# Seven half-size products for eight in the up-projections of a block's two feed-forward layers

## The chip, the cores and the metric

The program runs on one core of a Trainium2 chip. The metric is the device time of one execution in microseconds (us), the median of three runs. The engines of the core work side by side, and each takes its own instructions strictly in the order of its queue: TensorE (PE in the profile, its weight loads PEld) multiplies matrices into PSUM banks; ScalarE (ACT) and VectorE (DVE) work element by element on SBUF and PSUM; GpSimd (POOL) does the same on SBUF here; SyncE (SP) issues the transfers of weights.

## The reference

Two transformer blocks over one sequence of 512 tokens and 1024 features, all in float32. The change concerns the second block, whose two feed-forward layers are

```python
D_FF = 2816
def swiglu(x, w_gu, w_down):
    g, u = jnp.split(x @ w_gu, 2, axis=-1)
    return (jax.nn.silu(g) * u) @ w_down

def second_block(x, ...):
    x = x + FFN_RES_WEIGHT * swiglu(rmsnorm_2(x, norm_ffn1_g[l]), ffn1_w_gu[l], ffn1_w_down[l])
    x = x + hybrid_mixer(rmsnorm_2(x, norm_mix_g[l]), w_in[l], ...)
    x = x + FFN_RES_WEIGHT * swiglu(rmsnorm_2(x, norm_ffn2_g[l]), ffn2_w_gu[l], ffn2_w_down[l])
    return rmsnorm_2(x, final_norm_g)
```

`x @ w_gu` is the up-projection (512 x 1024 by 1024 x 5632), the product with `w_down` the down-projection.

## The kernel before

**Products.** Activations stand as [feature, token], eight tiles of 128 features. A float32 value is held as two float32r parts, `h` and `l`, with h + l the value, and a product is three matmuls per tile of 128 input features: h by h, h by l, l by h (lines 274, 275 and 277 of `fm`). The weights are the stationary operand, the activations the moving one of 512 tokens (256 where a step runs by token halves).

**Weights.** `w_dma` loads blocks of 1024 x 256 (1 MB, tile `raw`, two buffers) on SP's queue. `w_split` cuts each in four chunks of 128 x 512: ACT copies a chunk into `wh` (line 186), DVE subtracts to get `wl` (line 187); there are three buffers of split blocks. A block's split is issued when `w_done` has freed a buffer.

**Feed-forward layer** (`ffn`). The 22 tiles of hidden features go in three rounds of 6, 8 and 8 (`ROUNDS`). In a round, each pair of tiles takes two blocks of weights, one of the g columns (called a here) and one of the u columns (v): 2 x 2 x 8 x 3 = 96 matmuls of 512 tokens. When a's bank is full ACT takes silu of it (line 946), when v's is full DVE multiplies with it (line 968), and `split` puts the result into the two parts `mh`, `ml` (ACT line 315, DVE line 318). Four down blocks then follow and add to x (DVE line 632), the last two of the last round by token halves with the next norm's squares: ACT squares, POOL adds them up (line 337). The first pair of a layer runs by token halves while the norm is still being finished; the other ten pairs of each layer run as written here.

**Order.** Instructions are issued in program order, and an engine runs them in that order. Side work (splits of weights, norms) is written as generators; `Weave` mixes their steps into the main stream by a clock `t` that counts the TensorE time that has been emitted. A generator says after each step how much of that clock is to pass until its next (1.6 for a chunk of a split, `MISC_D[0]`). Where the main stream needs a block whose split is not yet all issued, `wait` issues what is left of it there and then.

## Time and profile before

| | us |
|---|---|
| Runs | 2775.51, 2780.48, 2782.68; median 2780.48 |
| Span of the profiled execution, first to last instruction | 2771.8 |
| Median less that span | 8.7 |
| Busy: PE, PEld, DVE, ACT, POOL | 2725.3, 2309.7, 1466.6, 1052.3, 280.1 |
| Six stretches with the pairs in question (20 pairs) | 446.1 |

The profiled execution is one execution on the chip; its own time is its span and what lies around it, which is taken as the 8.7 us by which the median of the runs is above the span. The page gives busy times of whole engines. What an edit costs is read from a stretch (a table of busy times by engine) and from the timeline, which shows single instructions with start and duration. The start of one matmul after another is the rate of TensorE; its listed duration overlaps with the next.

### The profile page before, as it was taken

To read this page: it belongs to the slowest core of one execution; us is meant where nothing else is said; L and a number is where in the kernel's file an instruction comes from. 1 tells how busy PE (TensorE), PEld (TensorE's weight loads), DVE (VectorE), ACT (ScalarE), POOL (GpSimd) and SP (SyncE) were. 2 spreads that over 40 slices of the span, in tenths; PEclk is the share of its full clock that TensorE was granted. 3 is DMA by queue.
4 is the path that set the end of the run, shared out by engine and by line. 5 is a ranking of instruction groups with operands and counts; after the bars stand their busy time and mean duration, and the time that the engine had idled before them with its cause. 6 is when DMAs were issued, how large, how long until landed. Compare 5 with 4: busy or idle time off the path is not lost.

```text
span 2771.8 us, 36529 instructions
## 1 busy us (share of the span) xinstructions
PE 2725.3 (98%) x14561; PEld 2309.7 (83%) x14561; DVE 1466.6 (53%) x2791; ACT 1052.3 (38%) x2044; POOL 280.1 (10%) x404
## 2 busy tenths in 40 slices
PE   6999999999999999999999999999999999999999
PEld 5988898888978888888889888897878987988888
DVE  7866567767544896544446333353455235533333
ACT  3323343323323895433334232343256333422222
POOL 3111110000101792000011000010000000100001
PEclk9999999999999999999999999999999999999999
DMA  7542126555231001233222322323433233232221
GB/s 251 185 152 71 59 92 198 175 175 182 79 107 61 1 2 64 97 100 106 91 92 84 99 91 97 102 63 108 105 78 88 54 89 105 77 101 96 92 92 60
DMA packets 254183, 278.69 MB, mean 101 GB/s; under 512 B 12952, under 2 KB 228397, under 8 KB 254013
## 3 DMA queue, kind: packets, MB, share of 16 engines
q1 hardware_dynamic: 226283, 233.21, 27.0%
q10 hardware_dynamic: 27730, 43.14, 4.8%
q8 instruction: 115, 1.88, 0.3%
q14 instruction: 55, 0.45, 0.1%
HBM read 274.23 MB, written 2.10 MB: 100 GB/s over the span
## 4 chain that ended last, share of the span: by engine, by line
PE 92%; DVE 4%; ACT 1%; POOL 1%; issue 1%; ACTq 0%; DMA 0%; DVEq 0%; POOLq 0%
PE pg L274 26%; PE pg L275 26%; PE pg L277 26%; PE pa L733 2%; PE pg L306 1%; PE pg L304 1%; PE pg L305 1%; PE pa L1279 1%; DVE w L546 1%; PE pa L1322 1%; PE pa L360 1%; PE pg L1238 1%; PE pg L1237 1%; PE pa L1048 1%; PE pa L344 1%
## 5 line engine op out<-in xcount | busy, mean ns | idle before, releaser
L187 DVE TENSOR_TENSOR wl<-raw,wh 128x512 fp32r<-128x512 f32 x842 | 571.1, 711 | 426.6 <-ACT wh L186 425.0
L274 PE MATMUL pg<-b,wh 128*128 128x512 f32 (+1 forms) x1856 | 672.6, 363 | 1.0 <-DVE w L968 1.0
L275 PE MATMUL pg<-b,wl 128*128 128x512 f32 (+1 forms) x1856 | 667.2, 360 | 0.0
L274 PE MATMUL pg<-hTh,wh 128*128 128x512 f32 (+3 forms) x1672 | 638.4, 383 | 1.8 <-ACT hTh L315 1.2
L275 PE MATMUL pg<-hTh,wl 128*128 128x512 f32 (+3 forms) x1672 | 633.1, 380 | 0.7 <-DVE wl L187 0.7
L277 PE MATMUL pg<-hTl,wh 128*128 128x512 f32 (+3 forms) x1672 | 621.5, 376 | 0.0
L186 ACT ACTIVATE wh<-raw 128x512 fp32r<-128x512 f32 x842 | 477.6, 619 | 279.8 <-PE pg L277 173.4
L277 PE MATMUL pg<-b,wh 128*128 128x512 f32 (+1 forms) x1472 | 523.9, 358 | 0.0
L275 PEld LDWEIGHTS pg<-b,wl 128*128 128x128 f32 x1856 | 348.8, 188 | 56.4
L274 PEld LDWEIGHTS pg<-b,wh 128*128 128x128 f32 x1856 | 348.6, 188 | 56.5 <-DVE w L968 1.4
L274 PEld LDWEIGHTS pg<-hTh,wh 128*128 128x128 f32 (+2 forms) x1672 | 313.4, 187 | 72.5 <-issue 4.6
L277 PEld LDWEIGHTS pg<-hTl,wh 128*128 128x128 f32 (+2 forms) x1672 | 310.4, 188 | 66.8 <-DVE hTl L318 0.4
L275 PEld LDWEIGHTS pg<-hTh,wl 128*128 128x128 f32 (+2 forms) x1672 | 313.5, 187 | 60.0 <-DVE wl L187 1.1
L277 PEld LDWEIGHTS pg<-b,wh 128*128 128x128 f32 x1472 | 275.2, 188 | 42.9
L337 POOL TENSOR_TENSOR w<-w,w 128x256 f32<-128x256 f32 (+1 forms) x78 | 78.1, 1006 | 1797.6 <-ACT w L336 1797.1
L315 ACT ACTIVATE b<-w 128x512 fp32r<-128x512 f32 (+1 forms) x112 | 67.4, 602 | 380.2 <-DVE w L968 314.8
L277 PE MATMUL pg<-hTh,wh 128*128 128x512 f32 (+1 forms) x384 | 142.9, 378 | 0.0
L968 DVE TENSOR_TENSOR w<-w,pg 128x512 f32<-128x512 f32 (+1 forms) x96 | 61.5, 641 | 146.7 <-PE pg L277 146.2
L318 DVE TENSOR_TENSOR b<-w,b 128x512 fp32r<-128x512 f32 (+1 forms) x112 | 73.3, 654 | 74.8 <-ACT b L315 74.8
L546 DVE SCALAR_TENSOR_TENSOR w<-w,cact,w 128x512 f32<-128x512 f32 x140 | 106.4, 760 | 4.2 <-DMA w<-in_ada_w_dram 3.6
L952 DVE SCALAR_TENSOR_TENSOR w<-pg,PT,w 128x511 f32<-128x511 f32 (+1 forms) x96 | 67.6, 704 | 75.6 <-ACT w L950 73.9
L632 DVE SCALAR_TENSOR_TENSOR x<-pg,mod,x 128x512 f32<-128x512 f32 (+1 forms) x80 | 50.5, 640 | 95.7 <-PE pg L277 90.7
(378 smaller groups left out, 2898.0 us busy)
## 6 DMA issues: line engine op xcount, KB each, us to landing
raw<-in_ffn_w_up_dram SPq DMA_DIRECT2D x44, 1024.0 KB
raw<-in_ffn_w_gu_dram SPq DMA_DIRECT2D x44, 1024.0 KB
w<-in_ada_w_dram ACTq DMA_DIRECT2D x160, 256.0 KB
raw<-in_ffn_w_down_dram SPq DMA_DIRECT2D x32, 1024.0 KB
raw<-in_w_in_dram SPq DMA_DIRECT2D x32, 1024.0 KB
raw<-in_hg_w_in_dram SPq DMA_DIRECT2D x16, 1024.0 KB
raw<-in_ffn_w_down_dram SPq DMA_DIRECT2D x16, 768.0 KB
raw<-in_nsa_w_in_dram SPq DMA_DIRECT2D x10, 1024.0 KB
```

The source lines that it names most:

```text
L186: nc.scalar.activation(h[:, k:e], raw[:, k:e], AF.Copy)
L187: nc.vector.tensor_tensor(l[:, k:e], raw[:, k:e], h[:, k:e].bitcast(F32), op=OP.subtract)
L274: mm(p[:mw, :n], h[:, k, c], xh[:, k, lo:hi], start=k == 0, stop=False)
L275: mm(p[:mw, :n], l[:, k, c], xh[:, k, lo:hi], start=False, stop=False)
L277: mm(p[:mw, :n], h[:, j, c], xl[:, j, lo:hi], start=False, stop=j == nk - 1)
L315: self.nc.scalar.activation(h, src, AF.Copy)
L318: self.nc.vector.tensor_tensor(l, src, h.bitcast(F32), op=OP.subtract)
L337: nc.gpsimd.tensor_tensor(acc[0][:, lo:hi], acc[0][:, lo:hi], sq[:, lo:hi], op=OP.add)
L546: nc.vector.scalar_tensor_tensor(acc, w, self.cact[:, k:k + 1], acc, op0=OP.mult, op1=OP.add)
L733: mm(p[:, c, :n], s["k"][:, cc], q, start=True, stop=True)
L952: nc.vector.scalar_tensor_tensor(c[:, lo + d:hi], p[:, :n - d], w(j), c[:, lo + d:hi], op0=OP.mult, op1=OP.add)
L968: nc.vector.tensor_tensor(s_[:, lo:hi], s_[:, lo:hi], p[:, :hi - lo], op=OP.mult)
```

## The change

In the ten pairs after the first of each of the second block's two feed-forward layers, the two blocks of a pair are no longer multiplied one by one. The matrix of weights is seen as 2 x 2 (a and v columns by the two halves of the 1024 input features), the activations as 2 x 2 (the halves of the input features by the two halves of the tokens), and the product is formed in Winograd's variant of Strassen's way, with seven products of quarter size in place of eight. One step per product, in the order A11, S1, S2, A12, S3, S4, A22 (`FACTORS`, names of the weight factor): 2 x 4 x 3 = 24 matmuls of 256 tokens each (`fm_fast`, lines 475 to 477), 168 for a pair of blocks (called a group below).

What comes with it:

- Sums of weights on POOL: X = a21 + a22 (line 218), a11 - a21 in place (line 219), X - a11 once S1 is split (line 240), a12 - X once S2 is split (line 243). X (`wsum`, 128 x 1024) has one buffer, so the next group's X is formed once S4 is split.
- Splits of weights on ACT and DVE (lines 267 and 268): seven factors of 2 chunks, 14 chunks for a group, where the pair had 8.
- Sums of activations once per layer (`fast_inputs`): POOL lines 425 and 445, DVE lines 444, 446 and 447, then splits, into the tiles b2 and b3.
- Evacuation of a group: three PSUM copies on ACT (lines 1121, 1124, 1127), four adds or products with a PSUM operand on DVE (lines 1129, 1132, 1134, 1139), two silu on ACT (lines 1130, 1135), one product on POOL (line 1136), then two splits (lines 485, 488). PSUM tile A takes four of the products one after the other, E two, F one.
- In the whole kernel: weights are loaded and split by half blocks, with six half buffers of each kind; one more transient tile; a smaller scratch for the issuing of transfers. As many bytes of weights are loaded.

The diff, cut to its core (edits that only pass on half blocks are left out):

```diff
-RAW_BUFS, HL_BUFS, W2_BUFS = 2, 3, 10
+RAW_BUFS, HL_BUFS, W2_BUFS = 6, 6, 11
+SUM_D, CHUNK_D, T_D = 2.6, 1.2, 1.2
...
+    def w_sums(self):
...
+        g = self.groups[self.g_sums]
+        tt = self.nc.gpsimd.tensor_tensor
+        a11, a21, a22 = (self.w_raw[g["load"] + i] for i in range(3))
+        g["X"] = self.t([128, 4, 256], "wsum")
+        tt(g["X"], a21, a22, op=OP.add)
+        tt(a21, a11, a21, op=OP.subtract)
+        g["sums"] = True
...
+    def w_after(self, p):
+        k = p["kind"]
+        if k == "raw":
+            return self.raw_free(p["load"])
+        g = p["g"]
+        tt = self.nc.gpsimd.tensor_tensor
+        raw = lambda i: self.w_raw[g["load"] + i]
+        if k == "S1":
+            tt(g["X"], g["X"], raw(0), op=OP.subtract)
+            self.raw_free(g["load"])
+        elif k == "S2":
+            tt(g["X"], raw(3), g["X"], op=OP.subtract)
+        elif k == "S4":
+            self.g_free += 1
+            self.w_sums()
+        elif k != "A11":
+            self.raw_free(g["load"] + dict(S3=1, A22=2, A12=3)[k])
...
+        p = self.pieces[i]
+        while p["kind"] != "raw" and p["kind"][0] == "S" and not p["g"]["sums"]:
+            yield None
+        if p["kind"] in ("S2", "S4"):
+            yield SUM_D
+        nk, ncol = p["nk"], p["n"]
+        src = self.w_source(p)
+        h = self.t([128, 4, 256], "wh", HL_BUFS, F32R)
+        l = self.t([128, 4, 256], "wl", HL_BUFS, F32R)
         self.w_hl[i] = (h, l)
         step = max(1, 512 // ncol)
         for k in range(0, nk, step):
             e = min(nk, k + step)
-            nc.scalar.activation(h[:, k:e], raw[:, k:e], AF.Copy)
-            nc.vector.tensor_tensor(l[:, k:e], raw[:, k:e], h[:, k:e].bitcast(F32), op=OP.subtract)
+            nc.scalar.activation(h[:, k:e, :ncol], src[:, k:e, :ncol], AF.Copy)
+            nc.vector.tensor_tensor(l[:, k:e, :ncol], src[:, k:e, :ncol], h[:, k:e, :ncol].bitcast(F32),
+                                    op=OP.subtract)
             if slow:
-                yield MISC_D[0]
+                yield MISC_D[0] if p["kind"] == "raw" else CHUNK_D
         self.w_split_i += 1
-        self.w_dma()
+        self.w_after(p)
...
+    def fast_inputs(self, X, tags, first, second):
+        nc = self.nc
+        xh, xl = X
+        th, tl = self.big(tags[0], F32R), self.big(tags[1], F32R)
+        two = lambda t: t.rearrange("p (i t) -> p i t", t=256)
+        def whole(k, lo, f):
+            nc.gpsimd.tensor_tensor(two(f), xh[:, k::4, lo:lo + 256].bitcast(F32), xl[:, k::4, lo:lo + 256].bitcast(F32),
+                                    op=OP.add)
+            return f
+        def run():
+            yield from self.wv.wait_in(first)
+            yield 1.5
+            left = []
+            store = self.t([128, 1024], "hmask")
+            for k in range(4):
+                left.append(whole(k, 0, store[:, k * 512:k * 512 + 512] if k < 2 else self.w2()))
+                yield T_D
+            yield from self.wv.wait_in(second)
+            yield 0.5
+            for k in range(4):
+                r, q = whole(k, 256, self.w2()), left[k]
+                yield T_D
+                a, b = self.w2(), self.w2()
+                tt = nc.vector.tensor_tensor
+                tt(a[:, 0:256], r[:, 0:256], q[:, 0:256], op=OP.subtract)
+                nc.gpsimd.tensor_tensor(a[:, 256:512], r[:, 256:512], r[:, 0:256], op=OP.subtract)
+                tt(b[:, 0:256], r[:, 256:512], a[:, 0:256], op=OP.subtract)
+                tt(b[:, 256:512], q[:, 256:512], b[:, 0:256], op=OP.subtract)
+                for i, f in enumerate((a, b)):
+                    self.split(th[:, i * 4 + k, :], tl[:, i * 4 + k, :], f)
+                    yield T_D
+        return (th, tl), self.wv.spawn(run())
+    def fm_fast(self, X, T, blocks, after):
+        mm = self.nc.tensor.matmul
+        x = lambda k0, lo: tuple((t, k0, lo) for t in X)
+        t = lambda k0, lo: tuple((u, k0, lo) for u in T)
+        steps = (("A11", x(0, 0), "A"), ("S1", t(0, 0), "E"), ("S2", t(4, 0), "A"), ("A12", x(4, 0), "F"),
+                 ("S3", t(0, 256), "A"), ("S4", x(4, 256), "E"), ("A22", t(4, 256), "A"))
+        self.fast_banks = self.fast_banks or [self.pg() for _ in range(4)]
+        self.fast_banks[:2] = self.fast_banks[1::-1]
+        place = dict(zip("AEF", self.fast_banks[1:]))
+        banks = {}
+        for p, (name, (h_, l_), b) in zip(self.w_get(*blocks), steps):
+            assert self.pieces[p]["kind"] == name
+            h, l = self.w_piece(p)
+            first = b not in banks
+            if first:
+                banks[b] = place[b]
+            for m in range(2):
+                o = banks[b][:, m * 256:m * 256 + 256]
+                c = slice(m * 128, m * 128 + 128)
+                for k in range(4):
+                    xh, xl = (u[:, k0 + k, lo:lo + 256] for u, k0, lo in (h_, l_))
+                    mm(o, h[:, k, c], xh, start=first and k == 0 and m == 0, stop=False, skip_group_check=True)
+                    mm(o, h[:, k, c], xl, start=False, stop=False, skip_group_check=True)
+                    mm(o, l[:, k, c], xh, start=False, stop=k == 3 and m == 1, skip_group_check=True)
+                    self.wv.pe(3 * 256 * 0.000424)
+            self.w_done((p,), 0.1)
+            after(name, banks)
...
+                out += [("S", *pair)] if fast and t else pair
...
+        def fast_group(a, t):
+            c = {}
+            f = slice(t - a, t - a + 2)
+            two = lambda w: w.rearrange("p (m t) -> p m t", t=256)
+            def late(lo, src):
+                yield 1.2
+                self.split(mh[:, f, lo:lo + 256], ml[:, f, lo:lo + 256], two(src))
+            def after(step, banks):
+                A, E, F = (banks.get(n) for n in "AEF")
+                if step == "A11":
+                    c["1"] = self.w2()
+                    nc.scalar.activation(c["1"], A, AF.Copy)
+                elif step == "S1":
+                    c["5"] = self.w2()
+                    nc.scalar.activation(c["5"], E, AF.Copy)
+                elif step == "S2":
+                    c["2"] = self.w2()
+                    nc.scalar.activation(c["2"], A, AF.Copy)
+                elif step == "A12":
+                    nc.vector.tensor_tensor(c["1"], c["1"], F, op=OP.add)
+                    nc.scalar.activation(c["1"], c["1"], AF.Silu)
+                elif step == "S3":
+                    nc.vector.tensor_tensor(c["5"], c["5"], A, op=OP.add)
+                elif step == "S4":
+                    nc.vector.tensor_tensor(c["2"], c["2"], E, op=OP.add)
+                    nc.scalar.activation(c["2"], c["2"], AF.Silu)
+                    nc.gpsimd.tensor_tensor(c["2"], c["2"], c["5"], op=OP.mult)
+                    pend.append(self.wv.spawn(late(256, c["2"]), 1.2))
+                else:
+                    nc.vector.tensor_tensor(c["1"], c["1"], A, op=OP.mult)
+                    pend.append(self.wv.spawn(late(0, c["1"])))
+            self.fm_fast(X, T, ((up, 0, 8, t * 128, 256), (up, 0, 8, DFF + t * 128, 256)), after)
...
+                if fast and not first:
+                    self.wv.wait(t_task)
+                    fast_group(a, t)
+                    continue
...
+            for task in pend:
+                self.wv.wait(task)
+            pend.clear()
+            self.fast_banks = None
...
+                 tags=("b2", "b3"))
```

**ACT's queue, second round of the first of the two layers, third pair, before.** Between two evacuations (line 946) ACT splits blocks for later pairs; `wh_13609` and `wh_13675` belong to the next pair.

```order
L186 ACTIVATE wh_13609<-raw_13524 128x512 x2
L946 ACTIVATE w_1604_13635<-pg_13602 128x512 [waits PE_49]
L186 ACTIVATE wh_13609<-raw_13524 128x512
L946 ACTIVATE w_1607_13666<-pg_13637 128x512 [waits PE_49]
L186 ACTIVATE wh_13675<-raw_13591 128x512 [waits DMAHW7_49,Activation_49]
L186 ACTIVATE wh_13675<-raw_13591 128x512 x2
L315 ACTIVATE b_1574_13330<-w_1604_13635 128x512 [waits DVE_49]
L186 ACTIVATE wh_13675<-raw_13591 128x512
L315 ACTIVATE b_1574_13330<-w_1607_13666 128x512 [waits DVE_49]
```

**The same place after, from the end of one group (its splits, line 485) through steps A11, S1 and S2 of the next.** `wsum_14473` is X of that next group; `wh_14549` is the split of S1, `wh_14609` that of S2, `pg` the PSUM tiles.

```order
L485 ACTIVATE b_1949_14071<-w_1983_14406 128x2x256 [waits Pool_49]
L267 ACTIVATE wh_14549<-wsum_14473 128x512 [waits Activation_49]
L485 ACTIVATE b_1949_14071<-w_1976_14338 128x2x256 [waits DVE_49]
L267 ACTIVATE wh_14549<-wsum_14473 128x512
L1121 ACTIVATE w_1998_14578<-pg_14073 128x512 [waits PE_49]
L1124 ACTIVATE w_2000_14607<-pg_14075 128x512 [waits PE_49]
L267 ACTIVATE wh_14609<-wsum_14473 128x512 [waits Pool_49]
L267 ACTIVATE wh_14609<-wsum_14473 128x512
L267 ACTIVATE wh_14619<-raw_14440 128x512 [waits DMAHW4_49,Activation_49]
L267 ACTIVATE wh_14619<-raw_14440 128x512
```

Between the S1 and the S2 step the copy of S1's product (line 1124, waiting for PE) now stands ahead of the split of S2's factor, which the very next step reads; before, the splits that stand here are read by the pair after.

**DVE's queue, before, in the same pair.** `wl_13676` belongs to the next pair's second block.

```order
L187 TENSOR_TENSOR wl_13676<-raw_13591,wh_13675 128x512 [waits DMAHW7_49,PE_49,Activation_49]
L187 TENSOR_TENSOR wl_13676<-raw_13591,wh_13675 128x512 [waits Activation_49] x2
L968 TENSOR_TENSOR w_1604_13635<-w_1604_13635,pg_13668 128x512 [waits PE_49]
L318 TENSOR_TENSOR b_1575_13331<-w_1604_13635,b_1574_13330 128x512 [waits Activation_49]
L187 TENSOR_TENSOR wl_13676<-raw_13591,wh_13675 128x512 [waits Activation_49]
L968 TENSOR_TENSOR w_1607_13666<-w_1607_13666,pg_13704 128x512 [waits PE_49]
L318 TENSOR_TENSOR b_1575_13331<-w_1607_13666,b_1574_13330 128x512 [waits Activation_49]
```

**The same place after, steps S3 to A22 of one group.** `wl_14708` is the lower part of S4's factor, `wl_14720` of A22's, `wl_14757` of the next group's A11.

```order
L268 TENSOR_TENSOR wl_14652<-raw_14271,wh_14651 128x512 [waits Activation_49] x2
L1129 TENSOR_TENSOR w_1998_14578<-w_1998_14578,pg_14076 128x512 [waits PE_49]
L1132 TENSOR_TENSOR w_2000_14607<-w_2000_14607,pg_14073 128x512 [waits PE_49]
L268 TENSOR_TENSOR wl_14708<-wsum_14473,wh_14707 128x512 [waits Activation_49] x2
L268 TENSOR_TENSOR wl_14720<-raw_14341,wh_14719 128x512 [waits DMAHW3_49,Activation_49]
L268 TENSOR_TENSOR wl_14720<-raw_14341,wh_14719 128x512 [waits Activation_49]
L1134 TENSOR_TENSOR w_2005_14646<-w_2005_14646,pg_14075 128x512 [waits PE_49]
L268 TENSOR_TENSOR wl_14757<-raw_14509,wh_14756 128x512 [waits DMAHW5_49,DVE_49,Activation_49]
L268 TENSOR_TENSOR wl_14757<-raw_14509,wh_14756 128x512 [waits Activation_49]
```

The add of S3's product (line 1132, waiting for PE) now stands ahead of the subtraction that makes S4's lower part, and S4 is the next step.

**POOL's queue, before, around the same layer: the last of the additions for the norm ahead of it, and the first for the norm behind it.** Nothing stands between them.

```order
L337 TENSOR_TENSOR w_1445_12072<-w_1445_12072,w_1494_12466 128x256 [waits Activation_49]
L337 TENSOR_TENSOR w_1443_12070<-w_1443_12070,w_1498_12511 128x256 [waits Activation_49]
L337 TENSOR_TENSOR w_1445_12072<-w_1445_12072,w_1499_12514 128x256 [waits Activation_49,Pool_49]
L337 TENSOR_TENSOR w_1695_14664<-w_1695_14664,w_1704_14733 128x512 [waits PE_49,Activation_49,Pool_49]
L337 TENSOR_TENSOR w_1695_14664<-w_1695_14664,w_1708_14770 128x512 [waits Activation_49,Pool_49]
L337 TENSOR_TENSOR w_1695_14664<-w_1695_14664,w_1711_14803 128x512 [waits Activation_49,Pool_49]
```

**After, one group's sums and its product.** `wsum` is X, `raw` the loaded quarter blocks.

```order
L218 TENSOR_TENSOR wsum_14473<-raw_14271,raw_14341 128x1024 [waits DMAHW2_49,DMAHW3_49,DVE_49,Pool_49]
L219 TENSOR_TENSOR raw_14271<-raw_14269,raw_14271 128x1024 [waits DMAHW1_49,Pool_49]
L1136 TENSOR_TENSOR w_1983_14406<-w_1983_14406,w_1978_14367 128x512 [waits Activation_49]
L240 TENSOR_TENSOR wsum_14473<-wsum_14473,raw_14269 128x1024 [waits DVE_49]
L243 TENSOR_TENSOR wsum_14473<-raw_14440,wsum_14473 128x1024 [waits DMAHW4_49,DVE_49,Pool_49]
L218 TENSOR_TENSOR wsum_14713<-raw_14511,raw_14581 128x1024 [waits DMAHW6_49,DMAHW7_49,DVE_49,Pool_49]
L219 TENSOR_TENSOR raw_14511<-raw_14509,raw_14511 128x1024 [waits DMAHW5_49,Pool_49]
```

Five instructions of POOL for each group stand where there was none, and the product of line 1136 stands behind the next group's two sums.

## Rows read from the trace of the kernel before

**Rows 1.** The page: busy by engine; clock; chain; the matmuls by lower parts (last: idle).

```profile
PE 2725.3 (98%) x14561; PEld 2309.7 (83%) x14561; DVE 1466.6 (53%) x2791; ACT 1052.3 (38%) x2044; POOL 280.1 (10%) x404
PEclk9999999999999999999999999999999999999999
PE 92%; DVE 4%; ACT 1%; POOL 1%; issue 1%; ACTq 0%; DMA 0%; DVEq 0%; POOLq 0%
L275 PE MATMUL pg<-hTh,wl 128*128 128x512 f32 (+3 forms) x1672 | 633.1, 380 | 0.7 <-DVE wl L187 0.7
```

**Rows 2.** Busy by stretch; columns PE, PEld, DVE, ACT, POOL, clock, DMA share, GB/s.

```profile
1577.10:1666.20 89.10, 89.10 (x385) 72.01 (x384) 30.39 (x47) 25.97 (x47) 0.00 (x0) 1.00 0.30 98
sum 446.10, PE 446.10 PEld 360.19 DVE 152.24 ACT 130.40 POOL 0.00; mean PE 74.35 PEld 60.03 DVE 25.37 ACT 21.73 POOL 0.00
```

**Rows 3.** Timeline of PE: start, us, what; matmuls of 512 tokens, four pairs.

```profile
1577.08 0.39 PE L274 MATMUL pg<-hTh,wh 128*128 128x512 f32 x1
...
1666.25 0.40 PE L274 MATMUL pg<-b,wh 128*128 128x512 f32 x1
```

**Rows 4.** Timeline of PE: matmuls of 256 tokens, first and last of two runs.

```profile
1448.21 0.28 PE L274 MATMUL pg<-b,wh 128*128 128x256 f32 x1
...
1461.52 0.28 PE L277 MATMUL pg<-b,wh 128*128 128x256 f32 x1
...
1490.07 0.29 PE L275 MATMUL pg<-hTh,wl 128*128 128x256 f32 x1
...
1492.59 0.29 PE L275 MATMUL pg<-hTh,wl 128*128 128x256 f32 x1
```

**Rows 5.** Timeline of ACT in the second round, from a pair's start.

```profile
1582.85 0.60 ACT L946 ACTIVATE w<-pg 128x512 f32<-128x512 f32 x1 [4.42 <-PE pg L277]
1583.35 1.14 ACT L186 ACTIVATE wh<-raw 128x512 fp32r<-128x512 f32 x2
...
1588.92 1.66 ACT L186 ACTIVATE wh<-raw 128x512 fp32r<-128x512 f32 x3
```

**Rows 6.** Timeline of DVE, the same stretch.

```profile
1577.28 0.69 DVE L632 SCALAR_TENSOR_TENSOR x<-pg,x 128x512 f32<-128x512 f32 x1 [2.23 <-PE pg L277]
1577.95 1.30 DVE L187 TENSOR_TENSOR wl<-raw,wh 128x512 fp32r<-128x512 f32 x2
1589.57 1.90 DVE L187 TENSOR_TENSOR wl<-raw,wh 128x512 fp32r<-128x512 f32 x3 [4.28 <-ACT wh L186]
1594.00 0.69 DVE L968 TENSOR_TENSOR w<-w,pg 128x512 f32<-128x512 f32 x1 [2.53 <-PE pg L277]
1595.99 0.68 DVE L187 TENSOR_TENSOR wl<-raw,wh 128x512 fp32r<-128x512 f32 x1
```

**Rows 7.** Timelines of ACT and DVE: from a copy's start to the subtraction behind it.

```profile
1661.60 0.63 ACT L315 ACTIVATE b<-w 128x512 fp32r<-128x512 f32 x1 [4.14 <-DVE w L968]
...
1662.26 0.69 DVE L318 TENSOR_TENSOR b<-w,b 128x512 fp32r<-128x512 f32 x1 [0.70 <-ACT b L315]
```

**Rows 8.** Timeline of POOL, elementwise instructions of two sizes.

```profile
40.69 6.17 POOL L542 TENSOR_TENSOR w<-w,w 128x512 f32<-128x512 f32 x4 [15.74 <-ACT w L540]
722.21 1.30 POOL L337 TENSOR_TENSOR w<-w,w 128x512 f32<-128x512 f32 x1 [4.20 <-ACT w L336]
1068.63 1.30 POOL L337 TENSOR_TENSOR w<-w,w 128x512 f32<-128x512 f32 x1 [16.76 <-ACT w L336]
1454.51 1.45 POOL L337 TENSOR_TENSOR w<-w,w 128x256 f32<-128x256 f32 x2 [1.53 <-ACT w L336]
```

**Rows 9.** Timeline of DVE beside and behind those instructions of POOL.

```profile
42.36 3.37 DVE L546 SCALAR_TENSOR_TENSOR w<-b,cact,w 128x512 f32<-128x512 f32 x2
47.18 5.47 DVE L546 SCALAR_TENSOR_TENSOR w<-b,cact,w 128x512 f32<-128x512 f32 x7
722.62 1.43 DVE L187 TENSOR_TENSOR wl<-raw,wh 128x512 fp32r<-128x512 f32 x1 [1.22 <-ACT wh L186]
1069.10 2.58 DVE L187 TENSOR_TENSOR wl<-raw,wh 128x512 fp32r<-128x512 f32 x3 [1.22 <-ACT wh L186]
```

## What the change is predicted to do

> **What bounds the kernel now.** I read the page first, then the six stretches that hold the pairs to be changed, then single instructions in them, then each pair of engines that would have to share work.
>
> The page says TensorE: busy for 98% of the span, 92% of the chain of waits, the full clock in each of the forty slices [rows 1]. In the six stretches this is complete: 446.10 us long, PE busy for 446.10, DVE for 152.24, ACT for 130.40, POOL not at all [rows 2]. Four pairs take 1666.25 - 1577.08 = 89.17 us [rows 3], so a pair takes 22.3 and a matmul of 512 tokens 0.2322. Here a microsecond of TensorE is one of the kernel, and there is room on the other engines: per pair some 14.7 us of DVE's and 15.8 of ACT's. What the change spends there is free only while it is done before TensorE asks for it. So I ask of each added instruction what it stands behind in its queue, and which step reads it.
>
> **The change part by part** (each term for both layers together; negative is faster).
>
> *Multiplications.* A matmul of 256 tokens starts every (1461.52 - 1448.21) / 113 = 0.1178 us with the operand b, and every (1492.59 - 1490.07) / 21 = 0.1200 with hTh and hTl [rows 4]. Four of the seven steps read the sums in b2 and b3, three read hTh and hTl: a mean of 0.1187, and 168 x 0.1187 = 19.95 us for a group. That is 2.36 under the pair, not the 2.79 of an eighth. Twenty groups: **-47.2**, between -43.0 (all at 0.1200) and -50.4 (all at 0.1178).
>
> A page makes this larger. "TensorE: Matmul & The Clock Gate" of the Trainium skill, section on the back-to-back issue gap, gives 262 cycles for 256 columns, an estimate of 0.109 us and 18.3 for a group; the rows of this kernel show 0.118 to 0.120, and I go by them. By the page the term would be about -80.
>
> *The wait ahead of S2.* A group's splits are paced at 7 x 2 x 1.2 + 2 x 2.6 = 22.0 us of the clock that issues them, while a group's matmuls advance that clock by 168 x 256 x 0.000424 = 18.2. The lead of the splits is lost by 3.8 per group, and the queue after the change shows where it ends: from a round's second or third group on, S2's split is issued at the end of S1, behind the copy of S1's product (line 1124). That copy starts 0.20 us after a step's last matmul (1577.08 to 1577.28 on DVE [rows 3, 6]), holds ACT for 0.50 (1582.85 to the next at 1583.35 [rows 5]), then S2's first chunk takes 0.62 (1.14 for two at a pitch of 0.52 [rows 5]) and 0.04 to cross. TensorE stands for about 1.4 us. The lower part, 0.69 more on DVE after 0.03 [rows 6, 7], is read two matmuls (0.24) later: 1.85. I take 1.7.
>
> *The wait ahead of S4.* Here DVE's add of S3's product (line 1132) is ahead of the subtraction for S4's lower part: 0.20 + 0.67 (1594.00 is 0.69 alone; two in a row take 0.61 to 0.67 each [rows 6]) + 0.69 - 0.24 = 1.3. I take 1.35. These two waits are 3.05 per steady group, more than the 2.36 gained: a steady group is 23.0 before anything is said of POOL.
>
> *POOL's chain to A11 and S1.* X has one buffer, so the next group's two sums begin when S4 is split, about 0.7 after S4 starts. POOL takes 1.30 for 128x512 and 0.72 for 128x256 [rows 8], so 128x1024 is about 2.45 by that slope, and 3.1 by the slowed row (6.17 for four, 1.54 each [rows 8]); the two sums take 4.9 to 6.2, the product of line 1136 behind them 1.3 to 1.54. Behind it ACT has the split of line 485 (0.6) ahead of S1's first chunk (0.6), and DVE has line 488 (0.7) and line 1139 ahead of its lower part (0.7). From S4's start that is 0.7 + 4.9 + 1.3 + 0.6 + 0.6 + 0.7 = 8.8 at the least and 11.5 at the most (DVE at its slowed times as well). S1 starts three steps after S4, at 3 x 2.85 = 8.55. So 0.3 to 3 us are waited; I take 1.9. The sum of line 240 (2.45 from S1's split) ends about when the copy of line 1124 does, and that of line 243 has two steps of room: both at nothing, with line 240 at 0.6 if POOL runs at its slowed rate.
>
> A steady group is then 19.95 + 1.7 + 1.35 + 1.9 = **24.9** against 22.3. Ten groups are steady (in each layer three of round two, two of round three): 10 x 4.95 = **+49.5**, between 10 x 3.05 = 30.5 and 10 x 7 = 70. Six (the second group of the first round and the first ones after it, as the lead runs out) have one of the two fixed waits: 6 x 1.35 = **+8.1**, from 0 to 18. Two have none.
>
> *First group of each layer.* Its S1 reads the sums of activations. Their last two thirds of work stand on POOL behind the sum of line 240: 2.45 + 3 x 0.72 + 2 x 1.30 = 7.2, then a DVE add and a split (0.4 + 0.6 + 0.7), and A11's step covers 2.85: 6.0. Twice: **+12**, from 6 to 16.
>
> *Ends of rounds.* The down blocks read `mh` and `ml`, whose last parts come from the product on POOL and line 1139; before, one split followed the last product. About 1.2 for each of six rounds (a split's two halves, 0.6 and 0.7): **+7**, from 0 to 12.
>
> *Norms.* The sums of the next layer's weights (two of 2.45 to 3.1) stand on POOL ahead of additions that the norm waits for, in two places: **+3**, from 0 to 6.
>
> *Everything else.* Half blocks, six buffers and the input sums' other parts leave the rest of the kernel with the same chunks and the same bytes. All idle time of the matmuls with lower parts that a split ended was 0.7 us [rows 1], so at most about that is to be gained; one wait of the S2 kind in each of three stages would cost 5. I take 0.
>
> Sum: -47.2 + 49.5 + 8.1 + 12 + 7 + 3 = **+32.4**. On the span of 2771.8 this gives 2804.2; the profiled execution's own time is 8.7 more, which is the median of the runs by the way it was taken, so 2804.2 + 8.7 = **2812.9, rounded to 2813 us**.
>
> **The rivals.**
>
> *A. The gain stays.* If ACT and DVE run ahead of TensorE by more than the issuing order says, the waits shrink. For it: DVE and ACT are idle for two thirds of these stretches [rows 2]. Against it: lines 1124 and 1132 wait for TensorE's step to end, and no engine passes an instruction of its own queue. With the fixed waits at a third and the rest at its lower bounds: -47.2 + 10 + 6 = -31, **2749 us**.
>
> *B. The two fixed waits alone.* POOL's chain fits in its three steps, since its lower estimate is only 0.3 over. -47.2 + 30.5 + 8.1 + 12 = +3.4, **2784 us**: the gain and the waits cancel.
>
> *C. POOL and DVE hold each other up.* One mechanism, at one place: an elementwise instruction of DVE with two SBUF operands stands nearly still while POOL runs one. It is in the trace. A subtraction of 0.69 took 1.43 beside a POOL instruction of 1.30, three that take 1.90 took 2.58 with 0.83 of them beside POOL, and two that take 0.78 each took 3.37, while POOL's own went from 1.30 to 1.54 [rows 6, 8, 9]. POOL would be busy for 4 x 2.45 + 1.3 = 11.1 of each group's 22, and DVE has 16 such instructions in a group. It decides where the subtractions for S2, S4 and S1 fall beside a sum: each then takes 0.75 more, and the chain to S1 is at its upper end. A steady group is 24.9 + 2 x 0.75 + 0.6 = 27.0 and the others about 1 more: 2813 + 21 + 10 = **2844 us**. Half of it is in my forecast by the middle values.
>
> "GPSIMD Engine Reference" of the Trainium skill, sections on specifications and engine selection, says the same in general: POOL shares its SBUF interfaces with DVE where DVE has two SBUF inputs, and elementwise work belongs on DVE. The trace agrees (1.43 for 0.69). It speaks against this change, and stands behind rival C.
>
> *D. It isn't seven eighths in time.* If a matmul of 256 tokens were held back by its weight load, 168 of them would save nothing. The rows that run so show 0.118 to 0.120 over 113 and 21 in a row [rows 4], so I give this no more than 0.02; at the 0.133 where nothing is gained the time would be 2813 + 47 = 2860 us.
>
> **How the numbers follow.** Forecast 0.45 (own range 2795 to 2830); A 0.17 (2733 to 2765); B 0.20 (2772 to 2795); C 0.16 (2830 to 2870); D 0.02. About 0.3%, 8.3 us, is what a measurement here can tell from no change: faster means under 2772, slower over 2789. Faster: A, and a seventh of B, 0.20. Same: 0.13, most of B. Slower: 0.67. To leave out no more than 2 in 10 the range reaches into the upper third of A and the lower half of C: 2755 to 2850.
>
> **What would show it.** In the changed kernel's stretches: starts of line 475 to 477 every 0.118 to 0.120 us inside a step; a gap of PE of 1.4 to 1.9 ahead of S2, ended by the split of line 267 or 268, with line 1124 just ahead of that on ACT; 1.3 ahead of S4 ended by line 268 behind line 1132; a gap ahead of S1 ended by the same lines behind POOL's line 1136; 4 to 8 us ahead of the first group's S1, ended by line 485 or 488. DVE's subtractions at 0.69 where POOL is idle and 1.4 beside it. The six stretches together near 446 + 32 = 478 us. I am wrong if the gaps ahead of S2 and S4 are under 0.5 us, if POOL's 128x1024 is far from 2.5 to 3.1, or if time appears in stages without these groups.

## The result: 70 us slower, and what the profile after shows

The changed kernel takes 2851.6 us (median of 4 runs, 2846.7 to 2854.4) against 2781.1 for the kernel before beside it: a ratio of 1.0261, 95% interval 1.0245 to 1.0276. The prediction was slower, 2813 us, with 2755 to 2850 as its range. The direction held; the loss was 70.5 us, not 32.4, and came out just above the range, where rival C (2844) stood. The two profiled spans differ by 78.6 us.

The page after (answers to [rows 1]) and the six stretches of the groups (answers to [rows 2]; last line, the sum of all six):

```profile
PE 2720.7 (95%) x16001; PEld 2365.3 (83%) x16001; DVE 1710.2 (60%) x3009; ACT 1162.2 (41%) x2258; POOL 545.7 (19%) x528
PEclk8999999999998999999998999999999999999999
```

```profile
1506.95:1567.51 60.56, 45.09 (x337) 42.76 (x337) 44.41 (x55) 25.08 (x47) 23.88 (x13) 0.86 0.18 57
1601.06:1700.94 99.88, 86.06 (x673) 80.93 (x672) 65.82 (x75) 43.77 (x80) 40.78 (x17) 1.00 0.27 85
...
sum 512.27, PE 433.19 PEld 410.15 DVE 350.59 ACT 218.95 POOL 200.52; mean PE 72.20 PEld 68.36 DVE 58.43 ACT 36.49 POOL 33.42
```

The stretches grew from 446.1 to 512.3 us, 66.2 of the 78.6. DVE is busy for 351 us in them where it was for 152; by the durations of [rows 6] its work for twenty groups is some 254 (14 subtractions at 0.61, six instructions at 0.69 in each), and the activation sums are the smaller part of the rest. In the first stretch of each layer the granted clock is 0.86. The largest waits of TensorE in the groups' matmuls (lines 475 to 477; us in total, times, longest):

```profile
PE pg L477 <- DVE wl L268: 41.3, 79, 1.8
PE pg L475 <- ACT b L485: 16.3, 5, 4.5
PE pg L475 <- ACT wh L267: 13.6, 12, 1.2
PE pg L476 <- DVE b L488: 5.1, 6, 2.2
```

The waits of one steady group, on PE's timeline (in brackets the idle time and what ended it): S2's two, A12's, S4's, A22's, A11's two and S1's.

```profile
1631.47 0.39 PE L475 MATMUL pg<-b,wh 128*128 128x256 f32 x1 [1.20 <-ACT wh L267]
1632.20 0.39 PE L477 MATMUL pg<-b,wl 128*128 128x256 f32 x1 [0.22 <-DVE wl L268]
1636.22 0.38 PE L477 MATMUL pg<-hTh,wl 128*128 128x256 f32 x1 [0.21 <-DVE wl L268]
1642.61 0.39 PE L477 MATMUL pg<-hTh,wl 128*128 128x256 f32 x1 [1.15 <-DVE wl L268]
1646.61 0.39 PE L477 MATMUL pg<-b,wl 128*128 128x256 f32 x1 [0.19 <-DVE wl L268]
1649.43 0.39 PE L477 MATMUL pg<-hTh,wl 128*128 128x256 f32 x1 [0.43 <-DVE wl L268]
1651.11 0.38 PE L477 MATMUL pg<-hTh,wl 128*128 128x256 f32 x1 [0.70 <-DVE wl L268]
1654.54 0.38 PE L477 MATMUL pg<-b,wl 128*128 128x256 f32 x1 [0.31 <-DVE wl L268]
...
1657.89 0.39 PE L475 MATMUL pg<-b,wh 128*128 128x256 f32 x1 [1.20 <-ACT wh L267]
```

From S2 to the next S2 it is 1657.89 - 1631.47 = 26.42 us. POOL and DVE in the same group:

```profile
1632.88 2.73 POOL L243 TENSOR_TENSOR wsum<-raw,wsum 128x1024 f32<-128x1024 f32 x1 [2.33 <-issue]
1643.29 2.71 POOL L218 TENSOR_TENSOR wsum<-raw,raw 128x1024 f32<-128x1024 f32 x1 [7.67 <-DVE wl L268]
1646.08 2.75 POOL L219 TENSOR_TENSOR raw<-raw,raw 128x1024 f32<-128x1024 f32 x1
1648.79 1.72 POOL L1136 TENSOR_TENSOR w<-w,w 128x512 f32<-128x512 f32 x1
```

```profile
1632.66 4.87 DVE L268 TENSOR_TENSOR wl<-raw,wh 128x512 fp32r<-128x512 f32 x4
...
1643.08 3.48 DVE L268 TENSOR_TENSOR wl<-raw,wh 128x512 fp32r<-128x512 f32 x2
1646.48 0.68 DVE L1134 TENSOR_TENSOR w<-w,pg 128x512 f32<-128x512 f32 x1
1648.37 2.69 DVE L268 TENSOR_TENSOR wl<-raw,wh 128x512 fp32r<-128x512 f32 x2 [1.22 <-ACT wh L267]
```

Two subtractions that take 1.30 [rows 6] take 3.48 across the sum of line 218. The first of them, already begun, takes its 0.68; the second takes 2.88 and ends 0.55 behind the sum, so it stands nearly still until POOL's instruction is over. Line 1134, with one operand in PSUM, takes its 0.68 in the middle of line 219.

The first group of a layer took 37.9 and 32.8 us. Its sums of activations on DVE, beside POOL's sums of lines 240 and 243, and TensorE in S1 (first layer):

```profile
1507.75 2.52 POOL L240 TENSOR_TENSOR wsum<-wsum,raw 128x1024 f32<-128x1024 f32 x1 [7.76 <-DVE wl L268]
...
1517.11 2.46 POOL L243 TENSOR_TENSOR wsum<-raw,wsum 128x1024 f32<-128x1024 f32 x1 [0.63 <-DVE wl L268]
```

```profile
1508.04 2.51 DVE L446 TENSOR_TENSOR w<-w,w 128x256 f32<-128x256 f32 x1
...
1517.41 2.45 DVE L446 TENSOR_TENSOR w<-w,w 128x256 f32<-128x256 f32 x1
1519.89 0.42 DVE L447 TENSOR_TENSOR w<-w,w 128x256 f32<-128x256 f32 x1
```

```profile
1511.85 0.39 PE L475 MATMUL pg<-b,wh 128*128 128x256 f32 x1 [1.43 <-ACT b L485]
...
1518.15 0.58 PE L475 MATMUL pg<-b,wh 128*128 128x256 f32 x1 [4.50 <-ACT b L485]
1520.98 0.58 PE L476 MATMUL pg<-b,wh 128*128 128x256 f32 x1 [2.25 <-DVE b L488]
...
1525.29 0.58 PE L475 MATMUL pg<-b,wh 128*128 128x256 f32 x1 [3.52 <-ACT b L485]
```

A subtraction of 128x256 that takes 0.42 (as line 447 does when the sum is over) takes 2.5 beside a sum. And the granted clock falls (columns as in [rows 2]):

```profile
1514.00:1516.00 2.00, 0.00 (x0) 0.00 (x0) 2.00 (x3) 0.00 (x0) 1.92 (x2) 0.50 0.00 0
...
1526.00:1528.00 2.00, 1.91 (x9) 1.91 (x10) 1.90 (x4) 2.00 (x5) 0.00 (x0) 0.50 0.00 0
1528.00:1530.00 2.00, 2.00 (x11) 2.00 (x11) 1.32 (x3) 1.18 (x3) 0.00 (x0) 0.50 0.35 94
1532.00:1534.00 2.00, 2.00 (x19) 2.00 (x19) 0.00 (x0) 1.03 (x3) 0.00 (x0) 1.00 0.21 75
```

TensorE was mostly idle from 1510 to 1526. The granted clock reads 0.50 (1.2 GHz) from 1514, and TensorE, busy again from 1526, ran at it until about 1530: 20 matmuls in 4 us where 19 stand in two later, some 2 us lost in the first group of a layer.

Outside the groups the largest single loss is at the first layer's norm. POOL's sums for the first group stand in its queue ahead of the additions of the norm's squares (line 507 here), and TensorE waits for these:

```profile
1459.52 2.41 POOL L218 TENSOR_TENSOR wsum<-raw,raw 128x1024 f32<-128x1024 f32 x1 [1.10 <-DMA raw<-in_ffn_w_gu_dram]
1462.01 2.73 POOL L219 TENSOR_TENSOR raw<-raw,raw 128x1024 f32<-128x1024 f32 x1
1464.70 2.77 POOL L507 TENSOR_TENSOR w<-w,w 128x256 f32<-128x256 f32 x4
```

```profile
1466.84 0.38 PE L514 MATMUL pa<-ones,w 128*128 128x128 f32 x1 [2.57 <-POOL w L507]
```

### The profile page after: what moved, and what is told of

It is laid out like the page before. It is cut to its first block, busy times and chain, and to the rows that moved or that the text cites. A ratio compares the mean times of both kernels' runs of the same rounds, so it can differ in the third digit from the quotient of the medians.

```text
span 2850.4 us, 40764 instructions
## 1 busy us (share of the span) xinstructions
PE 2720.7 (95%) x16001; PEld 2365.3 (83%) x16001; DVE 1710.2 (60%) x3009; ACT 1162.2 (41%) x2258; POOL 545.7 (19%) x528
## 5 line engine op out<-in xcount | busy, mean ns | idle before, releaser
L268 DVE TENSOR_TENSOR wl<-raw,wh 128x512 fp32r<-128x512 f32 (+1 forms) x860 | 674.7, 818 | 298.7 <-ACT wh L267 296.4
L267 ACT ACTIVATE wh<-raw 128x512 fp32r<-128x512 f32 (+1 forms) x860 | 481.0, 610 | 179.6 <-PE pg L378 138.0
L375 PE MATMUL pg<-hTh,wh 128*128 128x512 f32 (+2 forms) x1032 | 386.5, 376 | 1.7 <-ACT hTh L485 1.2
L376 PE MATMUL pg<-hTh,wl 128*128 128x512 f32 (+2 forms) x1032 | 380.6, 371 | 0.7 <-DVE wl L268 0.5
L378 PE MATMUL pg<-hTl,wh 128*128 128x512 f32 (+2 forms) x1032 | 372.0, 368 | 0.0
L375 PEld LDWEIGHTS pg<-hTh,wh 128*128 128x128 f32 (+1 forms) x1032 | 194.1, 188 | 43.0 <-issue 4.6
L378 PEld LDWEIGHTS pg<-hTl,wh 128*128 128x128 f32 (+1 forms) x1032 | 190.8, 188 | 37.8 <-DVE hTl L488 0.4
L376 PEld LDWEIGHTS pg<-hTh,wl 128*128 128x128 f32 (+1 forms) x1032 | 194.0, 188 | 33.1 <-DVE wl L268 1.1
L475 PE MATMUL pg<-b,wh 128*128 128x256 f32 x640 | 183.8, 287 | 31.5 <-ACT b L485 16.3
L477 PE MATMUL pg<-b,wl 128*128 128x256 f32 x640 | 184.7, 289 | 11.6 <-DVE wl L268 11.6
L476 PE MATMUL pg<-b,wh 128*128 128x256 f32 x640 | 182.0, 284 | 5.1 <-DVE b L488 5.1
```

Source lines behind the costliest of these rows:

```text
L267: nc.scalar.activation(h[:, k:e, :ncol], src[:, k:e, :ncol], AF.Copy)
L268: nc.vector.tensor_tensor(l[:, k:e, :ncol], src[:, k:e, :ncol], h[:, k:e, :ncol].bitcast(F32), op=OP.subtract)
L375: mm(p[:mw, :n], h[:, c], xh[:, k, lo:hi], start=k == 0, stop=False)
L376: mm(p[:mw, :n], l[:, c], xh[:, k, lo:hi], start=False, stop=False)
L378: mm(p[:mw, :n], at(j)[0][:, c], xl[:, j, lo:hi], start=False, stop=j == nk - 1)
L475: mm(o, h[:, k, c], xh, start=first and k == 0 and m == 0, stop=False, skip_group_check=True)
```

## The experiments

Two theories stood against each other. ORDER: the waits come from the issuing order. LOCK: DVE can't run an instruction with two SBUF operands while POOL runs one. Beside them stand LOAD (ACT and DVE simply have too much to do) and, for the layers' first groups, FIRST (the chain of activation sums and the lower clock behind it). Ratios are to the kernel before, measured beside each run; over 1 is slower. "Groups" below is the time of all groups, each from the start of its A11 to the first matmul behind its A22 (512.3 us for twenty as changed; 384.7 for sixteen with a plain first round).

**Split ahead of the evacuation.**

```diff
+        prev = None
...
             h, l = self.w_piece(p)
+            if prev:
+                after(prev, banks)
...
-            after(name, banks)
+            prev = name
+        after(prev, banks)
```

> In each group the split of the next step's factor is issued ahead of the evacuation of the step before, instead of behind it; nothing else changes. Changed kernel: steady group 26.42 us, of it S2 3.43 and S4 4.24 where 2.83 and 2.84 would be free of waits, and S1 4.78. Theory ORDER (the gaps ahead of S2 and S4 come from the issuing order alone): both go, 1.9 + 1.4 us, steady group about 23.1, ten of them give 33 us, time about 2818. Theory LOCK (DVE cannot run a subtraction of two SBUF operands while POOL runs a sum, and X's second form ends only at 1656.97, 0.25 us ahead of where ACT is free anyway): S4's gap goes, S2's stays at 1.0 or more, and part of what S4 gives comes back ahead of A11 and S1; steady group 24.7 to 25.3, time 2836 to 2845.

Measured: ratio 1.0223 (1.0194 to 1.0253), groups 504.4 us. The wait ahead of S4 is gone (its step takes 2.86 instead of 4.24), that ahead of S2 is not, and A22 takes 5.6 to 7.1 instead of 3.3: the time came back there, and not ahead of A11 and S1 where I had put it. For its factor two subtractions take 5.34 across the sums of lines 218 and 219. Steady groups 22.2 to 28.1, 25.1 in the mean. LOCK fits, ORDER doesn't.

**No sums of weights.** S1, S2 and S4 are split from loaded blocks; lines 218, 219, 240 and 243 are left out.

> Leaves out the sums of weights on POOL (lines 218, 219, 240, 243); S1 and S2 are split from a21 and S4 from a22 instead, so the result is not the reference's. Matmuls, splits, evacuations and their order stay. LOCK: what stops A12, A22, A11 and S1 (0.47 + 0.44 + 1.65 + 0.56 us of a steady group, with the refill of the pipeline) is DVE's subtractions held up by POOL's sums, so these go, and the gaps ahead of S2 (1.9) and S4 (1.4), which come from the order, stay: steady group 23.3, time about 2852 - 10 x 3.1 - 6 x 1.5 - 5 = 2807. Rival LOAD (ACT and DVE are simply late with 14 chunks and six evacuations): the small gaps stay, steady group 25.5 to 26.4, time over 2840.

Measured: 1.0087 (1.0058 to 1.0116), groups 468.3, steady 24.1 us: 44 of the 66 us are gone. A12 and A22 are back at 2.85 and 2.83, so what stopped them was the sums (this run alone can't say whether by the lock or by when they end); S2 and S4 keep their waits, 1.20 with 0.22 and 1.15. What is left over 23.3 is 0.37 of idle time in A11: the product on POOL (1.29) still holds up two subtractions there (2.04 instead of 1.30).

**Sums on DVE.** `gpsimd` becomes `vector` in `w_sums` and `w_after`.

> The four sums of weights of a group run on DVE in place of POOL; the order of issue is the same. A 128x1024 sum on DVE is estimated at 1.25 us (0.69 for 128x512, 0.61 one behind the other), 5 us more of DVE's time in a group of 20. LOCK: no subtraction is held up any more and X is ready 1.2 us sooner each time: the gaps of A12, A22, A11 and S1 shrink to less than half, steady group 23.3 to 24.5, time 2815 to 2830. Rival LOAD (DVE's queue is the bound): DVE has 5 us more in the same chain, steady group 26.5 or more, time 2852 or more.

Measured: 1.0167 (1.0138 to 1.0197), groups 483.9, steady 24.3 to 25.4; the groups a bit above LOCK's range and clearly under LOAD's. A12 is free of waits; A22, where the next group's sums now stand in DVE's own queue, is not (3.7). DVE has four sums more in its queue and the groups take 28 us less for it.

**First round plain.**

```diff
-                out += [("S", *pair)] if fast and t else pair
+                out += [("S", *pair)] if fast and t >= 6 else pair
...
-                if fast and not first:
+                if fast and t >= 6:
```

> The two pairs of each layer's first round that had seven products are multiplied as before the change (eight, 22.3 us each); the other 16 groups stay, so the sums of activations on POOL have the first round to be done in. The four groups took 37.9, 22.7, 32.8 and 27.5 us, 120.9 together, and would take 89.2. Theory FIRST (their cost is the chain of activation sums and the lower clock behind it): 32 us go, time about 2820, all other groups as they were. Rival (the chain is only moved on, the second round's first group then waits): less than 16 us go, time over 2836.

Measured: 1.0104 (1.0069 to 1.014), span 2800.8, 49.6 under the changed kernel's. The four groups give their 32 us, the sixteen behind 6.7 more (391.4 to 384.7). From 500 matmuls ahead of the first layer to the end of its first pair the changed kernel had taken 103.1 us where the kernel before took 98.1; now it is 100.3, since TensorE no longer waits there for POOL's additions. Some 6 of the 49.6 lie ahead of that, where the two kernels don't differ, and belong to no term. FIRST holds for its 32.

**Splits sooner** (`SUM_D, CHUNK_D` from 2.6, 1.2 to 1.4, 0.9), alone and with the first round plain.

> Only two numbers change: a chunk's pause from 1.2 to 0.9 and the pause ahead of S2 and S4 from 2.6 to 1.4, so that a group's splits are paced at 7 x 2 x 0.9 + 2 x 1.4 = 15.4 us of the issuing clock, under the 18.2 of its matmuls, and stay some steps ahead. ORDER alone: the gaps ahead of S2 and S4 and the chain to S1 go, steady group 20.0 to 20.6, time about 2852 - 10 x 5.7 - 6 x 2 = 2783. LOCK sets a floor that pacing can't move: POOL's five instructions hold DVE off its two-operand work for 4 x 2.7 + 1.5 = 12.3 us of a group, and DVE's own such work (14 subtractions and two of line 488 at 0.61 to 0.69) takes 9.9, so a group can't be under about 22.2: time 2810 to 2820. The first group of each layer keeps its 33 to 38 us in both.

> The sooner splits, and the first round's pairs multiplied as before the change. The sum of what the two give alone if they don't meet: e5 stood at 1.0104 of the kernel before, some 2805, and 8 steady groups of 25.4 to 26.4. ORDER: those at 20.0 to 20.6, 16 groups 325 us instead of 385, time 2745. LOCK: groups at the floor of 22.2, 355 us, time 2775, level with the kernel before (22.3 per pair).

Measured: 1.0242 (1.0221 to 1.0262) and 1.0068 (1.0046 to 1.0089); groups 510.3 and 380.9, next to nothing gained. Both expectations missed. ORDER's missed by far. LOCK's floor of 22.2 is no bound for a single group (the second kernel's take 21.2 to 27.2), and their mean of 23.8 stays above it. What TensorE waits for has changed: in the second kernel 31.0 us for line 1121 and 15.2 for line 1132, the evacuations. In one of its groups:

```profile
1620.14 3.50 DVE L268 TENSOR_TENSOR wl<-raw,wh 128x512 fp32r<-128x512 f32 x2
1623.57 0.67 DVE L1134 TENSOR_TENSOR w<-w,pg 128x512 f32<-128x512 f32 x1
...
1630.36 0.39 PE L475 MATMUL pg<-b,wh 128*128 128x256 f32 x1 [1.91 <-ACT w L1121]
```

Now the splits stand ahead of the evacuations, and a split that the sum of line 243 holds up (3.50) holds up line 1134, then silu, the product on POOL, line 485 and line 1121, which A's next matmul waits for. Pacing only chooses who is late behind a locked instruction.

**Splits sooner, first round plain, sums on DVE.**

> As the one before it, with the sums of weights on DVE too. DVE then has 14 x 0.61 + 2 x 0.69 + 4 x 0.69 + 4 x 1.25 = 17.7 us of work in a group of 19.95, and POOL only one product of 1.3. LOCK: the floor of 22.2 is gone, groups 20.0 to 20.8, 16 groups 326 us, time 2805 - 59 = about 2746, faster than before by 1%. Rival LOAD (DVE at 89% of a group can't keep its lead): groups over 22, time 2775 or more.

Measured: 0.9906 (0.9889 to 0.9922), 2751.7 us, groups 334.2 (20.2 to 21.5 each), 8 over LOCK's 326: in half of them TensorE still waits about 1.0 for line 1121. One sum takes 1.23 on DVE, and the two subtractions behind it are back at 1.29:

```profile
1640.66 1.23 DVE L243 TENSOR_TENSOR wsum<-raw,wsum 128x1024 f32<-128x1024 f32 x1
1641.80 1.29 DVE L268 TENSOR_TENSOR wl<-raw,wh 128x512 fp32r<-128x512 f32 x2
```

Over the same sixteen groups the pace alone gave 4 us beside a plain first round (384.7 to 380.9) and 9 without it (391.4 to 382.3); the move alone gave 17 without it (391.4 to 374.7) and was not run beside it. Both together gave 50 (384.7 to 334.2). Either cause is enough to keep TensorE waiting.

**Sums in quarters on POOL**, four instructions of 128x256 for each, otherwise as the kernel with sooner splits and a plain first round.

> As the kernel with sooner splits and a plain first round (16 groups, 380.9 us; time 1.0068 of before), but each sum of 128x1024 on POOL is issued as four of 128x256 (0.72 to 0.74 us each in the trace of before). POOL's work grows from 2.7 to about 3 us per sum. LOCK as exclusion for the length of one POOL instruction: a subtraction caught beside a sum waits 0.75 instead of up to 2.7, and DVE gets a turn between the quarters, so chunks that took 2.7 to 3.5 us for two take 2.2 to 2.9; the 16 groups shrink by 10 to 30 us to 350 to 370. Rival (DVE and POOL share a rate, so that only the sum of their work counts): nothing is gained, 380 to 395 us.

Measured: 0.9993 (0.9981 to 1.0004), groups 360.0, 21 us less for the same sums on the same engine.

```profile
1617.80 4.19 POOL L247 TENSOR_TENSOR wsum<-raw,wsum 128x256 f32<-128x256 f32 x4 [0.63 <-DVE wl L272]
```

```profile
1618.24 0.85 DVE L272 TENSOR_TENSOR wl<-wsum,wh 128x512 fp32r<-128x512 f32 x1
1619.01 2.38 DVE L272 TENSOR_TENSOR wl<-raw,wh 128x512 fp32r<-128x512 f32 x2
```

(Lines 247 and 272 are lines 243 and 268 here.) The sum takes 4.19 instead of 2.73, because DVE now gets its turns between; two subtractions take 2.38 instead of 3.50. A shared rate would have gained nothing; this is exclusion for the length of one instruction.

**No products changed**, the rest of the change kept.

> All of the change's machinery of half blocks, six buffers and one more transient tile, but every pair multiplied as before the change. The changed kernel lost 12 us outside its groups, 6 of them around the first layer's norm. Theory: those come from POOL's sums and the activation sums around the norm, so this kernel is level with the one before, 2772 to 2783. Rival: the half blocks themselves cost them, 2786 or more.

Measured: 0.9991 (0.998 to 1.0001). Half blocks and six buffers cost nothing that can be measured.

**Alignment**, in the kernel before and in the best one, then the product of line 1136 on DVE as well.

```diff
-        self.eps = self.t([128, 1], "eps")
+        self.eps = self.t([128, 9], "eps")[:, :1]
...
-        self.mod = self.t([128, 96], "mod")
+        self.mod = self.t([128, 104], "mod")[:, :96]
...
-        r = self.t([128, 4], "rstd", 6)
+        r = self.t([128, 4], "rstd", 7)
```

> The kernel before, with three small tiles enlarged so that hTh and hTl (and x and the transient tiles) start at a multiple of 64 bytes of a partition instead of 32 over one; nothing else changes. Matmuls of 512 tokens ran every 0.2322 us with hTh or hTl as operand and every 0.2290 with b0, 256 tokens at 0.1200 and 0.1178; b0 to b3 and the weights stand at multiples of 64. Theory ALIGN: the rate with hTh and hTl becomes that with b0; some 4500 matmuls by 0.0032 are 14 us, time 2763, 0.5% faster. Rival (the rate comes from something else, as the source of the tiles or what the other engines do beside them): no change, 2775 to 2780.

> The best kernel so far (sooner splits, first round plain, sums of weights on DVE: 0.9906 of before, 2752) with the same three tiles enlarged. ALIGN: fewer matmuls with hTh and hTl are left in 512 tokens, so somewhat less than in the kernel before, 10 to 13 us: 2740. Rival: 2752.

> As the one before it, with the product of line 1136 on DVE as well, so that POOL has nothing left in a group. In the best kernel so far TensorE still waits 1.0 us in half of the groups for the copy of A11's product (line 1121), which stands on ACT behind line 485, which waits for this product (1.3 to 1.4 us on POOL with a subtraction of DVE held up beside it, 2.0 instead of 1.3 for two). On DVE it is 0.69. The chain is 0.6 to 1.2 us shorter: 8 groups by 0.6 to 1.0 us, 5 to 8 us, time 2733. Rival: DVE at 18.4 of 20 us is late elsewhere, no change or slower.

Measured: 0.9922 (0.9904 to 0.994), 0.9845 (0.9829 to 0.986) and 0.9825 (0.9808 to 0.9841), 2731.4 us, 1.75% under the kernel before. The last one's sixteen groups take 329.4 us (333.6 with the product on POOL); with 4 us less in the groups and 5 in all it stands at the lower end of what was expected. In the kernel before so aligned, 14 matmuls with hTh and hTl start in 1574.91 - 1571.70 = 3.21 us, 0.2293 each, where it was 0.2322 [rows 3]:

```profile
1571.70 0.39 PE L274 MATMUL pg<-hTh,wh 128*128 128x512 f32 x1
...
1574.91 0.39 PE L277 MATMUL pg<-hTl,wh 128*128 128x512 f32 x1
```

Matmuls with b kept their pace: the 144 of a first round's down blocks take 32.97 us before and 32.96 here. So the rate goes with the operands that were moved. That they stood 32 bytes past a multiple of 64 is read from the order of allocation; no trace shows an address.

So the seven products are worth 0.9825 / 0.9922 = 0.990 where their sums don't lock DVE, on sixteen of twenty groups.

## Why the prediction was right in direction and wrong in size

By its own terms, in us of the two profiled spans:

| Term | Forecast | Measured | Of it without the sums of weights |
|---|---|---|---|
| Multiplications | -47.2 | -48.5 (19.88 a group) | -48.5 |
| Ten steady groups | +49.5 | +61.6 (mean 26.04) | +42.0 (24.08) |
| Six with one wait | +8.1 | +20.0 | +5.4 |
| Two with none | 0 | +2.1 | 0.0 |
| First groups | +12 | +30.9 | +23.3 |
| Outside the groups (ends, norms, rest) | +10 | +12.4 | +4.9 |
| Sum | +32.4 | +78.6 | +27.0 |

The last column is the run that leaves the sums of weights out; four of its groups wait for nothing and take 19.84 to 19.89, from which the first row is taken.

- *Direction*: right for the reason given. Without any sum of weights the waits of the steady groups already take back most of what the multiplications give, and the first groups the rest: that run is slower than the kernel before, at 1.0087.
- *Multiplications, the waits ahead of S2 and S4*: right, in place, size and what ended them. A matmul of 256 tokens starts every 0.118 us inside a step; S2's wait is 1.20 and 0.22, S4's 1.15, behind lines 1124 and 1132. The -80 that the prediction sets beside its term compares a price that no row shows with a measured pair; the sum does not use it. That order alone could have these waits back, the experiments refuted.
- *The step that failed* is the price of POOL's sums of weights. The sum has them as a chain: 1.9 us ahead of S1 in ten steady groups (19), 2.45 in each first group, 3 at the norms, and nothing for DVE's subtractions in the other groups. Left out, they give back 44.0 us in the groups: 19.6 in the steady ones, 14.6 in the six, 2.1 in the two, 7.6 in the first ones. I had the lock as rival C, at 0.75 for a subtraction, from rows where POOL's instruction takes 1.30 [rows 8, 9], and put half of it into the forecast by "middle values", which in the sum are that 1.9. It lasts as long as POOL's instruction, here 2.4 to 2.75: a subtraction of 0.68 took 2.88. In [rows 9] it could be read: 2.58 for three beside 0.83 of POOL is 0.68 more, nearly all of it.
- *What was luck.* In the steady groups 19 was forecast for 19.6, but not where it came. The chain to S1 was to cost 1.9 there; S1 waits 0.56, A11 about 1.65 (some 0.6 of it stays without the sums), A12 0.47 in each group and A22 0.46 in six of the ten, the last three at subtractions held up beside POOL. C's mechanism was right and its time, 2844, nearest, but its steady group of 27.0 is 1 us too long and its first groups are hardly longer than the forecast's.
- *First groups*: mis-sized by 18.9, and 11.3 of that stays without the sums of weights. I counted POOL's chain and one split at the end. There are three rounds from DVE to ACT and back, one for each tile still missing, with the first pair's own last evacuations (lines 1180, 485, 488) between them in DVE's queue, the lock on top, and some 4 us lost to the lower clock in the two layers. Without the sums of weights the two groups still took 32.1 and 31.0 us, so most of it is that chain; how it divides between queue and clock was not taken apart.
- *Outside the groups*: the size is near, the parts are not. The six ends of rounds took 0.6 each, 3.6 where 7 was forecast. The first layer's norm took 5.0: some 2.8 because the additions stand behind POOL's sums, as forecast (3, in two places), and most of the rest because two instructions of DVE were caught beside the activation sums of line 425 (1.57 and 1.05 us instead of 0.69 and 0.16). Another 2.5 lie ahead of the layer, at a matmul that kernels alike up to there reach anywhere between 1396 and 1404 us; no term is to be read from it.
- *Each short wait costs more than its listed idle time.* The eight of the steady group add up to 4.41 us, but the group is 26.42 - 19.88 = 6.54 over: 0.27 more each, in the matmul ahead of the gap (listed at 0.28, with 0.12 from start to start) and the first one behind it (the next start 0.22 later instead of 0.12). Over the hundred waits of the four rows shown first that would be some 27 us; this is an estimate.
- *The own time around the span*: I took 8.7 us. The run profiled after took 2852.2 for a span of 2850.4, so it is 1.8, and the profiled execution of before was, it seems, some 7 us under the median of its runs. This is most of the 8 us between the two sums, 78.6 and 70.5.

## What to carry to other kernels

Elementwise work moved to POOL is not free because POOL is idle: price it by the instructions of DVE with two SBUF operands that will be caught beside it, each for the rest of the POOL instruction. A plan that frees TensorE's time and spends it on operands made just in time is worth what the queue order lets be made early, and order and lock have to be solved together: alone they gave 4 to 9 us and 17, together 50. Sum the waits by starts of matmuls, not by listed idle time.

## What the runs showed of the hardware

- POOL's two-operand instructions and DVE's with two SBUF operands exclude each other for the length of one instruction (on DVE 0.42 became 2.51 beside 2.52 of POOL; in quarters, DVE's subtractions and POOL's additions take turns and a sum of four takes 4.19 instead of 2.73). DVE's with a PSUM operand (0.68) and ACT's copies (0.62) did not slow down beside them.
- The moving operand's address seems to matter: matmuls of 512 tokens started every 0.2322 us from hTh and hTl and every 0.2293 after the shift, while those from b kept their pace; the whole kernel gained 0.8%. Transient tiles and x were shifted too, so what share of the gain is TensorE's was not separated.
- The granted clock fell to 0.50 (1.2 GHz) while TensorE stood mostly idle in a layer's first group, and matmuls of 256 tokens then started every 0.21 us instead of 0.12 until it rose.
